# The last third of a gated MLP's down projection by seven block products, with the up tiles woven in another order

## The chip, the core and the metric

One core of a Trainium2 chip runs the whole kernel. The metric is device time in microseconds (us) of one execution. The median of three runs of the kernel before is 827.56 us (827.38 to 827.99). Engines go by their short names: PE is TensorE (matmul), DVE is VectorE, ACT is ScalarE, POOL is GpSimd, SP is SyncE, which issues most DMAs.

## The reference, cut to what matters

One inference step of a decoder layer: a mixer, cross-attention, then a gated MLP, and a final RMSNorm. The change lies in the MLP and the final norm. There are 512 prompt tokens and 8 sample tokens, 520 columns in all, held as two halves of 260.

```python
def conv_ffn(xn, prefix, w_up, conv_w, conv_b, w_down):
    up = xn @ w_up                      # 1024 -> 2 * 2816
    ext = jnp.concatenate([prefix, up], axis=1)
    c = conv_b
    for k in range(CONV_W): c = c + conv_w[k] * ext[:, k:k + T]     # causal, width 3
    gate, val = jnp.split(c, 2, axis=-1)
    return (jax.nn.silu(gate) * val) @ w_down, ext[:, -(CONV_W - 1):]   # 2816 -> 1024
```

## The kernel before, in words

Activations are held transposed, with 128 features on the partitions and 2 x 260 token columns. Every fp32 operand is split into two fp32r parts, hi (ACT, a copy that rounds) and lo (DVE, the difference: `split`, lines 117 and 120), and a product is three matmuls: hi.hi, hi.lo, lo.hi. Nearly every matmul is 128 x 128 weights against 260 columns.

The hidden layer has 22 tiles of 128 features (`FT`). An up tile j gives gate and value for both halves. Tiles 0 to 6 are **classic**: 8 blocks of the contraction, three matmuls each, two halves, two outputs, 96 matmuls. Tiles 7 to 21 go by **seven products** (`up_seven`, line 1870): gate and value, even and odd contraction blocks, and the two halves of the tokens form a 2 x 2 by 2 x 2 block product, done as seven block products instead of eight, 84 matmuls. The operands are sums of weight blocks and sums of activation blocks. The activation sums are made once (`mixes`, line 1738) and read through `xm`. Of the weight sums, two per tile are added by an accumulating DMA from POOL's queue (`both`, line 1877) and two by DVE (`sum2`, `sum4`, lines 1924 and 1929), each as the first thing of a later product's preparation. After the products, an up tile runs through `conv` (line 1674: two ACT and three DVE instructions) and `gate` (line 1689: Silu on ACT, gate times value on DVE, then the hi and lo split of the hidden tile).

The down projection reads the hidden tiles in three parts, `PARTS = ((0, 7), (7, 15), (15, FT))`, for each of 8 output blocks d (`down`, line 1859): classic, and added to the residual `hT` by DVE (line 1864). Parts 0 and 1 are placed between up tiles, one block d to an up tile, the rest behind the last one. Part 2 ends the stage: blocks d = 0 to 3 as `last_down` (line 1969), which also squares the finished block into an accumulator (`add_square`: ACT, then POOL, lines 274 and 276) and scales it (`final_block`); blocks 4 to 7 in the tail (lines 2055 to 2092), half by half, so that the first half's norm (`half_norm`) and stores (`half_store`) run beside the second half's matmuls.

The order is a list of `Step`s, written out by hand (lines 1941 to 1980). A step is a weight unit of up to 4 blocks (512 columns): loaded up to 13 steps ahead by SP into a ring of 13 raw units, split (`prep`) 3 steps ahead into a ring of 4 split units, and multiplied. In the seven-product stretch a step is 12 matmuls. After each step, two pieces of the deferred `conv` and `gate` work are issued (`POPS`, line 2007). Within each engine a list scheduler at build time orders ready instructions by priority, which is program order unless raised.

PSUM has three double banks `pp` and two single ones `t`. An up tile by seven products holds one `pp` and one `t`. The four outputs are read while products are still added: for instance product 6 adds onto the bank that products 1 and 5 left and that `keep` (line 1898) copies out first.

The `for m` loop from line 1991 drives it:

```python
    for m in range(-AHEAD, len(steps)):
        while loaded < min(m + EARLY, len(loads)) and loads[loaded].load():
            loaded += 1
        ...
        if m + AHEAD < len(steps):
            steps[m + AHEAD].prep()
        ...
        steps[m].mm()
        for _ in range(POPS):
            ...
```

Of the kernel before, what the change touches and what calls it, by code (L numbers as in the profile page):

```python
# [9 lines left out]
F32 = mybir.dt.float32  # L10
# [22 lines left out]
FT = DFF // P  # L33
MEM = 256
# [73 lines left out]
def decoder_step(ctx: ExitStack, tc: tile.TileContext, A, O):  # L108
# [1514 lines left out]
    w_up = A["w_up"][0]  # L1623
    w_down = A["w_down"][0]
    PARTS = ((0, 7), (7, 15), (15, FT))
    NA = PARTS[1][0]
    hid = {}
    hid_mid = []
    xs3 = blocks(x3_hi, x3_lo)
# [14 lines left out]
    def up_cols(v, j):  # L1644
        return slice(v * DFF + j * P, v * DFF + (j + 1) * P)

    def up_products(j):

        raws = [raw_w[j % 2][:, 2 * v:2 * v + 2].rearrange("p u (k c) -> p (u k) c", c=P) for v in range(2)]
        for v in range(2):  # L1650
            sp.dma_start(raws[v], w_up[:, up_cols(v, j)].rearrange("(k p) c -> p k c", p=P))
# [37 lines left out]
    def gate(j):  # L1689
# [6 lines left out]
        yield  # L1696
        tt(g, g, u, OP.mult)
        yield
        if NA <= j < PARTS[2][0]:
            if not hid_mid:  # L1700
                hid_mid.extend(ptile(ab3, [P, KT, 2, HT], t, F32R, name="h_mid") for t in ("x3_hi", "x3_lo"))
            hid[j] = tuple(t[:, j - NA] for t in hid_mid)
        else:
            hid[j] = tuple(ptile(ff, [P, 2, HT], t, F32R, bufs=7) for t in ("h_hi", "h_lo"))
# [25 lines left out]
    NI = KT // 2  # L1730
    xm4 = [ptile(actp, [P, 4, NI, HT], "act_a", F32R, bufs=2, name="xm4") for _ in range(2)]
    xm3 = ptile(ff, [P, 2, 3, NI, HT], "xm3", F32R)
    B11, B21, B22, T3_, N1, N2, T4_ = range(7)
# [25 lines left out]

    mix = mixes()  # L1760
# [28 lines left out]
    class Step:  # L1789

        def __init__(self, mm, load=None, prep=None, post=None, held=False):
            self.load_, self.prep_, self.mm_, self.post_, self.held = load, prep, mm, post, held
# [11 lines left out]
        def prep(self):  # L1804
            raw = self.prep_() if self.prep_ else self.raw
            if self.load_ and not self.held:
                self.free()
            n = raw.shape[1]
            self.w = tuple(t[:, :n] for t in ring_units(1))
            split(self.w[0], self.w[1], raw)  # L1810

        def mm(self):
            self.mm_(self.w)
            if self.post_:
                self.post_()

    def classic(ps_of, src, xs, kt, post):

        out = []
        for k0 in range(0, kt, 4):  # L1820
# [11 lines left out]
            out.append(Step(mm, load=lambda k0=k0, n=n: load_unit(rows(src, k0, n), n), post=post if k0 + n == kt else None))  # L1832
# [12 lines left out]
    def up_classic(j):  # L1845
        out = []
        for v in range(2):
# [8 lines left out]
            out.append(classic(ps, w_up[:, up_cols(v, j)], xs3, KT, post))  # L1856
        return out[0] + out[1]

    def down(pi, d, then=None):
# [8 lines left out]
        return classic(ps, w_down[j0 * P:j1 * P, d * P:(d + 1) * P], lambda k: hid[j0 + k], j1 - j0, post)  # L1868

    def up_seven(j):  # L1870

        ac, bb = held("pp"), held("t")

        def block(m, s):
            return w_up[:, up_cols(m, j)].rearrange("(i s p) c -> p s i c", s=2, p=P)[:, s]
# [38 lines left out]

        def out21():
            acopy(exts[j][:, 1, 0, 2:], a_of(False), scale=-1.0)
            behind.extend((conv(j, 1), gate(j)))

        s = {}
        s[1] = Step(product(a_of, B11, True), lambda: load_unit(block(0, 0)), held=True)  # L1920
        s[5] = Step(product(c_of, N1, True), both(block(1, 0), block(1, 1)), post=keep, held=True)
        s[2] = Step(product(b_of, B21, True), lambda: load_unit(block(0, 1)), post=out11, held=True)

        def sum2():
            tt(s[1].raw, s[1].raw, s[5].raw, OP.add)
            s[5].free()
            return s[1].raw

        def sum4():
# [244 lines left out]
```

## Time and profile before

| | |
|---|---|
| median of three runs | 827.56 us (827.38 to 827.99) |
| the profiled execution's own time | 827.17 us |
| its span, first to last instruction | 825.5 us |
| granted clock of PE, mean | 0.996 |
| PE / DVE / ACT busy, share of the span | 98% / 73% / 54% |
| matmuls | 6891 |

The busy share says how long an engine had something in it. Whether an engine sets the end is read from the chain of waits and from how fast its instructions follow one another. "L1890" is line 1890 of the kernel; a line of a helper (117, 120) stands for many uses, which the tile names tell apart.

### The profile page before, as it was taken

To read this page: it belongs to the slowest core of one execution; us is meant where nothing else is said; L and a number is where in the kernel's file an instruction comes from. 1 tells how busy PE (TensorE), PEld (TensorE's weight loads), DVE (VectorE), ACT (ScalarE), POOL (GpSimd) and SP (SyncE) were. 2 spreads that over 40 slices of the span, in tenths; PEclk is the share of its full clock that TensorE was granted. 3 is DMA by queue.
4 is the path that set the end of the run, shared out by engine and by line. 5 is a ranking of instruction groups with operands and counts; after the bars stand their busy time and mean duration, and the time that the engine had idled before them with its cause. 6 is when DMAs were issued, how large, how long until landed. Compare 5 with 4: busy or idle time off the path is not lost.

```text
span 825.5 us, 17791 instructions
## 1 busy us (share of the span) xinstructions
PE 808.3 (98%) x6891; PEld 753.7 (91%) x6891; DVE 605.2 (73%) x1460; ACT 447.9 (54%) x940; POOL 95.3 (12%) x100
## 2 busy tenths in 40 slices
PE   9999999899999999999999999999999999999996
PEld 8998878877778899999799999999999999999995
DVE  6644686887657776888673799997888887887714
ACT  6741347667665553444343465666666656665541
POOL 2300111000000031000032000111111111100021
PEclk9999999999999999999999999999999999999998
DMA  9988975833222283677443224756866866754422
GB/s 327 304 257 289 411 285 182 270 115 116 77 77 53 64 254 106 202 251 254 137 115 103 77 78 126 154 134 152 165 143 147 168 145 142 160 135 121 171 110 104
DMA packets 146366, 137.87 MB, mean 167 GB/s; under 512 B 6417, under 2 KB 133265, under 8 KB 144089
## 3 DMA queue, kind: packets, MB, share of 16 engines
q1 hardware_dynamic: 127224, 114.63, 44.5%
q0 software_dynamic: 18624, 21.26, 12.0%
q8 instruction: 54, 0.88, 0.4%
q10 hardware_dynamic: 432, 0.84, 0.3%
q14 instruction: 32, 0.25, 0.1%
HBM read 129.56 MB, written 10.69 MB: 170 GB/s over the span
## 4 chain that ended last, share of the span: by engine, by line
PE 90%; DVE 3%; ACT 3%; DMA 2%; issue 1%; SPq 0%; DVEq 0%; ACTq 0%
PE ps_pp L205 29%; PE ps_pp L1890 16%; PE ps_pp L1829 16%; PE ps_t L1890 3%; PE ps_tb L1266 3%; PE ps_o L1155 2%; PE ps_pp L2070 2%; PE ps_tb L1072 2%; PE ps_sc L1108 2%; PE ps_tf L1140 2%; PE ps_x L1467 1%; PE ps_tb L1234 1%; PE ps_x L1488 1%; ACT prob L1118 1%; PE ps_s L1528 1%
## 5 line engine op out<-in xcount | busy, mean ns | idle before, releaser
L1890 PE MATMUL ps_pp<-xm,w_hi 128*128 128x260 f32 x720 | 133.3, 285 | 0.0
L1890 PEld LDWEIGHTS ps_pp<-xm,w_hi 128*128 128x128 f32 x720 | 110.9, 188 | 2.3 <-ACT ext L117 0.2
L117 ACT ACTIVATE w_hi<-w_u 128x512 fp32r<-128x512 f32 (+2 forms) x110 | 72.7, 661 | 66.4 <-PE ps_pp L1890 22.7
L1890 PE MATMUL ps_pp<-xm,w_lo 128*128 128x260 f32 x360 | 101.5, 282 | 0.0
L120 DVE TENSOR_TENSOR w_lo<-w_u,w_hi 128x512 fp32r<-128x512 f32 (+2 forms) x110 | 80.1, 729 | 16.6 <-ACT w_hi L117 15.3
L1890 PEld LDWEIGHTS ps_pp<-xm,w_lo 128*128 128x128 f32 x360 | 67.7, 188 | 0.0
L120 DVE TENSOR_TENSOR hT<-hT,ps_pp 128x520 f32<-128x520 f32 (+1 forms) x44 | 28.4, 645 | 45.0 <-PE ps_pp L205 17.9
L205 PE MATMUL ps_pp<-x_hi,w_hi 128*128 128x260 f32 x288 | 59.9, 286 | 0.0
L205 PE MATMUL ps_pp<-x_hi,w_lo 128*128 128x260 f32 x288 | 59.6, 285 | 0.0
L205 PE MATMUL ps_pp<-x_lo,w_hi 128*128 128x260 f32 x288 | 58.5, 284 | 0.0
L117 ACT ACTIVATE w_hi<-w_raw 128x1024 fp32r<-128x1024 f32 (+1 forms) x38 | 35.1, 922 | 41.3 <-PE ps_pp L205 30.0
L1118 ACT ACTIVATE prob<-prob,mx 128x384 f32<-128x384 f32 (+3 forms) x64 | 35.4, 555 | 19.3 <-DVE mx L1116 19.1
L120 DVE TENSOR_TENSOR w_lo<-w_raw,w_hi 128x1024 fp32r<-128x1024 f32 (+1 forms) x38 | 41.4, 1089 | 6.1 <-ACT w_hi L117 5.8
L205 PEld LDWEIGHTS ps_pp<-x_hi,w_lo 128*128 128x128 f32 x288 | 44.9, 188 | 0.6 <-issue 0.4
L205 PE MATMUL ps_pp<-xn_hi,w_hi 128*128 128x260 f32 x208 | 45.1, 291 | 0.2 <-issue 0.2
L205 PEld LDWEIGHTS ps_pp<-x_hi,w_hi 128*128 128x128 f32 x288 | 44.9, 188 | 0.3
L1880 POOL DMA_DIRECT2D w_u<-in_w_up_dram x19 | 24.4, 1286 | 178.9 <-DMA w_u<-in_w_up_dram 106.8
L205 PEld LDWEIGHTS ps_pp<-x_lo,w_hi 128*128 128x128 f32 x288 | 44.4, 188 | 0.4 <-issue 0.4
L120 DVE TENSOR_TENSOR w_lo<-raw_x,w_hi 128x512 fp32r<-128x512 f32 (+1 forms) x53 | 35.7, 674 | 10.3 <-ACT w_hi L117 9.6
L205 PE MATMUL ps_pp<-xn_lo,w_hi 128*128 128x260 f32 x208 | 42.9, 285 | 0.3 <-DVE xn_lo L129 0.3
L205 PE MATMUL ps_pp<-xn_hi,w_lo 128*128 128x260 f32 x208 | 43.0, 286 | 0.0
L117 ACT ACTIVATE w_hi<-raw_x 128x512 fp32r<-128x512 f32 (+1 forms) x53 | 32.8, 618 | 18.1 <-PE ps_pp L1890 13.1
(495 smaller groups left out, 2309.8 us busy)
## 6 DMA issues: line engine op xcount, KB each, us to landing
w_u<-in_w_up_dram SPq DMA_DIRECT2D x57, 256.0 KB, 3.2
xkr<-in_cache_mem_dram SPq DMA_DIRECT2D x16, 512.0 KB, 4.7
xvr<-in_cache_mem_dram SPq DMA_DIRECT2D x16, 512.0 KB, 7.1
raw_x<-in_w_up_dram SPq DMA_DIRECT2D x26, 256.0 KB, 3.4
Kt<-in_k_t_dram SPq DMA_DIRECT2D x48, 128.0 KB, 3.2
w_u<-in_w_up_dram SPq DMA_DIRECT2D x10, 512.0 KB, 4.3
w_u<-in_w_down_dram SPq DMA_DIRECT2D x20, 256.0 KB, 4.4
w_u<-in_w_up_dram POOLq DMA_DIRECT2D x19, 256.0 KB, 5.8
```

The source lines that it names most:

```text
L117: act.activation(o, i, AF.Copy, scale=scale)
L120: (eng or dve).tensor_tensor(o, a, b, op=op)
L205: pe.matmul(o, a[:, k, :], x[:, hf, :], start=(k == 0 and j == 0), stop=(k == kt - 1 and j == 2))
L1072: pe.matmul(ps[:, :HT], a[:, k, :], y[x][:, k, hf, :], start=(k + j == 0), stop=(k == 3 and j == 2))
L1108: pe.matmul(ss_[hl][:, 0:n], Qst[:, h, qc], k[:, g, u, 0:n], start=(u == 0), stop=(u == 1), skip_group_check=True)
L1118: act.activation(p[:, 0:nk], p[:, 0:nk], AF.Exp, bias=mx[:, hh:hh + 1], scale=-1.0, accum_out=sm[:, hh:hh + 1])
L1140: pe.transpose(pt[:, hh * P:(hh + 1) * P], pr[hh][:, kb * P:(kb + 1) * P], ident)
L1155: pe.matmul(po[hp * 64:(hp + 1) * 64, g * 256:(g + 1) * 256], Vtok[:, br, kb, g * 64:(g + 1) * 64], pTs[kb][:, hp * 256:(hp + 1) * 256], s ...
L1266: pe.matmul(ps[i], x[:, k, ts_], w[:, kl, :], start=(k == 0 and j == 0), stop=(k == KT - 1 and j == 2))
L1829: pe.matmul(ps[:, hf, :HT], a[:, k, :], x[:, hf, :], start=(k0 + k + j == 0), stop=(k0 + k == kt - 1 and j == 2))
L1880: pool.dma_start(u[1], b, accum_op=OP.add)
L1890: pe.matmul(ps, a[:, i, :], b, start=(first and i + q == 0), stop=(i == NI - 1 and q == 2), skip_group_check=True)
```

## The change

- The down projection's parts become (0, 7), (7, 14), (14, 22). Its last part, eight hidden tiles, goes by seven products for output blocks 0 to 5, in three pairs (`down_seven`); blocks 6 and 7 stay classic, in the tail.
- Hidden tiles 14 to 21 are kept unsplit (`raw_hid`); `hidden_mixes` makes their block sums and the hi and lo parts, in pieces of four per step behind the up tiles.
- The steps of the up tiles are woven so that products of three tiles alternate (`weave`); `keep` joins `out11`; results are read out under high priority; the down blocks of part 0 stand with the first eight tiles, three of part 1 within the last tile, five behind it.
- The weight sums by DVE (`add`) follow the split of their own unit (`after`) instead of opening a later preparation. The accumulating DMAs are issued up to five steps after the load (`LATER`). The flag `dma`, which would give the other sums to POOL's queue as well, is False in both uses.
- The weights of up and down are laid out on the host so that a unit is one contiguous run per partition.
- The tail has two blocks instead of four; its weights are split in the last four steps; the first half's norm comes after the fourth contraction block of d = 6, its stores within d = 7. Three copies of cache and state from DRAM to DRAM (lines 1996 to 1999) wait until no accumulating DMA is left. Three pieces of deferred work follow a step instead of two.

The diff, cut to its core:

```diff
+PARTS = ((0, 7), (7, 14), (14, FT))
+DOWN_ORDER = list(range(14)) + list(range(14, FT, 2)) + list(range(15, FT, 2))
...
-    PARTS = ((0, 7), (7, 15), (15, FT))
-    xs3 = blocks(x3_hi, x3_lo)
+    def xs3(k):
+        kk = 2 * (k % NI) + k // NI
+        return x3_hi[:, kk], x3_lo[:, kk]
...
+        if j >= NB2:
+            if not raw_hid:
+                raw_hid.append(ptile(ff, [P, KT, 2, HT], "hA", name="raw_hid"))
+            tt(raw_hid[0][:, j - NB2], g, u, OP.mult)
+            yield
+            return
...
+        for i in range(NI):
+            e, o = raw_hid[0][:, 2 * i], raw_hid[0][:, 2 * i + 1]
+            both = raw_hid[0][:, 2 * i:2 * i + 2].rearrange("p s r t -> p r s t")
+            at_ = [t[:, :, i].rearrange("p (r s) t -> p r s t", r=2) for t in blk]
+            acopy(at_[0], both)
+            yield
+            n, t = (ptile(ff, [P, 2, HT], "cv", bufs=3, name="hz") for _ in range(2))
+            tt(n[:, 0], e[:, 0], e[:, 1], OP.subtract)
+            yield
+            tt(t[:, 0], o[:, 1], e[:, 1], OP.subtract)
+            yield
+            dve.scalar_tensor_tensor(n[:, 1], n[:, 0], -1.0, o[:, 1], op0=OP.mult, op1=OP.subtract)
+            acopy(mid[:, 0, 2, i], t[:, 0])
+            yield
+            dve.scalar_tensor_tensor(t[:, 1], n[:, 1], -1.0, o[:, 0], op0=OP.mult, op1=OP.subtract)
+            acopy(mid[:, 0, 0:2, i], n)
+            yield
+            tt(at_[1], both, at_[0].bitcast(F32), OP.subtract)
+            acopy(end[:, 0, i], t[:, 1])
+            yield
+            tt(mid[:, 1, 0:2, i], n, mid[:, 0, 0:2, i].bitcast(F32), OP.subtract)
+            yield
+            tt(mid[:, 1, 2, i], t[:, 0], mid[:, 0, 2, i].bitcast(F32), OP.subtract)
+            yield
+            tt(end[:, 1, i], t[:, 1], end[:, 0, i].bitcast(F32), OP.subtract)
...
             split(self.w[0], self.w[1], raw)
+            if self.after:
+                self.after()
 
         def mm(self):
             self.mm_(self.w)
             if self.post_:
-                self.post_()
+                with tc.high_priority():
+                    self.post_()
...
-                pool.dma_start(u[1], b, accum_op=OP.add)
+                adds.append([LATER, u[1], b])
...
         def sum2():
-            tt(s[1].raw, s[1].raw, s[5].raw, OP.add)
             s[5].free()
             return s[1].raw
 
         def sum4():
-            tt(s[2].raw, s[2].raw, s[1].raw, OP.add)
             s[1].free()
             s[2].free()
             return s[2].raw
 
-        s[6] = Step(product(a_of, N2, False), prep=sum2, post=lambda: acopy(exts[j][:, 0, 1, 2:], a_of(False)))
-        s[3] = Step(product(c_of, B22, False), prep=sum4, post=out12)
-        s[7] = Step(product(a_of, T3_, False), both(block(0, 0), block(1, 0)), post=out22)
-        s[4] = Step(product(a_of, T4_, False), lambda: load_unit(block(1, 1)), post=out21)
+        s[1] = Step(product(a_of, B11, True), lambda: load_unit(block(0, 0)), held=True)
+        s[5] = Step(product(c_of, N1, True), both(block(1, 0), block(1, 1)), held=True, after=lambda: add(1, 5))
+        s[2] = Step(product(b_of, B21, True), lambda: load_unit(block(0, 1)), post=posts[2], held=True, after=lambda: add(2, 1))
+        s[6] = Step(product(a_of, N2, False), prep=sum2, post=posts[6])
+        s[3] = Step(product(c_of, B22, False), prep=sum4, post=posts[3])
+        s[7] = Step(product(a_of, T3_, False), both(block(0, 0), block(1, 0)), post=posts[7])
+        s[4] = Step(product(a_of, T4_, False), lambda: load_unit(block(1, 1)), post=posts[4])
...
+        def add(m, r, x, op=OP.add):
+            tt(hT[:, d + m, r], hT[:, d + m, r], x(), op)
+
+        def first():
+            add(0, 0, a)
+            add(1, 1, c, OP.subtract)
+            add(0, 0, b)
+
+        def done():
+            add(1, 0, a, OP.subtract)
+            then(d)
+            then(d + 1)
+
+        posts = {2: first, 6: lambda: add(0, 1, a), 3: lambda: add(0, 1, c), 7: lambda: add(1, 1, a, OP.subtract), 4: done}
+        return seven(lambda m, s: w_down[d + m, :, NB2 + NI * s:NB2 + NI * s + NI], hm, ac, bb, posts, False)
...
-    steps += [sevens[0][i] for i in (1, 5, 2, 6, 3)]
-    for n, s in enumerate(sevens):
-        t = sevens[n + 1] if n + 1 < len(sevens) else None
-        if n:
-            steps += downs.pop(0)
-        if not t:
-            steps += [s[7]] + downs.pop(0) + [s[4]]
-        elif n:
-            steps += [s[7], t[1], t[5], s[4], t[2], t[6], t[3]]
-        else:
-            steps += [t[1], t[5], s[7], t[2], s[4], t[6], t[3]]
+    steps += [sevens[0][i] for i in (1, 5, 2)]
+    def weave(rows, places, last):
+
+        prev = None
+        for n, s in enumerate(rows):
+            t = rows[n + 1] if n + 1 < len(rows) else None
+            seq = ([s[6], t[1]] if prev and t else [t[1], s[6]] if t else [s[6]]) + ([prev[4]] if prev else [])
+            if t:
+                seq += [s[3]] + (downs.pop(0) if n in places else []) + [t[5], t[2], s[7]]
+            else:
+                seq += last() + [s[3]] + last() + [s[7]] + last() + [s[4]]
+            steps.extend(seq)
+            prev = s
+
+    weave(sevens, (0, 1, 2, 3, 4, 5, 6, 7), lambda: downs.pop(0))
+    ups_end = len(steps)
...
-    D0 = 4
-        steps += last_down(d)
+    D0 = 6
+    groups = [down_seven(q, down_done) for q in range(D0 // 2)]
+    steps += [groups[0][i] for i in (1, 5, 2)]
+    weave(groups, (), lambda: [])
...
-    AHEAD, EARLY, POPS = 3, 13, 2
+    AHEAD, EARLY, POPS = 3, 13, 3
...
+        soon = [s.raw for s in steps[max(m + AHEAD, 0):m + AHEAD + 4] if hasattr(s, "raw")]
+        for e in list(adds):
+            e[0] -= 1
+            if e[0] <= 0 or any(e[1] is r for r in soon):
+                adds.remove(e)
+                pool.dma_start(e[1], e[2], accum_op=OP.add)
         if m + AHEAD < len(steps):
             steps[m + AHEAD].prep()
         if m < 0:
             continue
+        if loaded == len(loads) and not adds and kept:
+            for o, i in kept:
+                with last_on(EN.SP):
+                    sp.dma_start(o, i)
+            kept = ()
...
+        if m >= ups_end:
+            for _ in range(4):
+                next(hidden, None)
+        if m >= len(steps) - 4 and hasattr(tail_raw[-1], "raw"):
+            tail_split(m - len(steps) + 4)
...
+                if hf == 1 and (d, k) == (D0, 4):
+                    stores = half_store(0, half_norm(0, sq0))
+                    lead = last_pe()
+                if hf == 1 and d == D0 + 1 and k in (1, 3, 5):
                     next(stores)
-                xhi, xlo = hid[j0 + k]
...
-            if hf == 1:
-                if d == D0:
-                    stores = half_store(0, half_norm(0, sq0))
...
+    given["w_up_t"] = x["w_up"][0].reshape(4, 2, P, 2, FT, P).transpose(3, 4, 2, 1, 0, 5)
+    given["w_down_t"] = x["w_down"][0].reshape(FT, P, KT, P).transpose(2, 1, 0, 3)[:, :, DOWN_ORDER]
```

## Rows read from the trace of the kernel before

**Rows 1.** The page, part 1: busy time of an engine, its share of the span, and its instructions.

```profile
PE 808.3 (98%) x6891; PEld 753.7 (91%) x6891; DVE 605.2 (73%) x1460; ACT 447.9 (54%) x940; POOL 95.3 (12%) x100
```

**Rows 2.** The chain that ended last, in order of time, in the MLP: start us, length us, what, and how many matmuls. Of the pieces like the one at 564.95 there are thirteen, one to an up tile, the last at 752.24. The last row is the end of the matmuls of the tail, but for the norm's.

```profile
536.60 7.37 PE ps_pp L1890 x60
...
545.41 3.14 PE ps_pp L1890 x24
...
549.54 1.71 PE ps_pp L1890 x12
...
562.55 1.45 PE ps_pp L1890 x12
...
564.95 1.63 PE ps_pp L1890 x12
...
752.24 1.64 PE ps_pp L1890 x12
...
767.29 25.89 PE ps_pp L1829 x216
...
809.38 5.76 PE ps_pp L2070 x48
```

**Rows 3.** Busy time of each engine in three stretches: three up tiles, each with a down block of 48 matmuls; the end of the up tiles with two more; and the classic last part before the tail. Columns: stretch, its length, then PE, PEld, DVE, ACT, POOL busy us (instructions), granted clock, DMA share, GB/s.

```profile
690.57:738.60 48.03, 48.03 (x398) 47.61 (x397) 39.55 (x70) 29.31 (x61) 6.44 (x5) 1.00 0.67 147
738.60:767.30 28.70, 28.70 (x240) 28.56 (x239) 20.68 (x36) 15.01 (x30) 0.00 (x0) 1.00 0.38 110
767.30:793.20 25.90, 25.90 (x218) 25.90 (x218) 13.79 (x24) 13.14 (x28) 4.43 (x4) 1.00 0.50 197
```

**Rows 4.** All groups of DVE instructions in the first of these stretches (690.57 to 738.60, three up tiles), by shape: count, busy us, mean ns of one, and the idle time before them with what ended it.

```profile
L120 DVE TENSOR_TENSOR w_lo<-w_u,w_hi 128x512 fp32r<-128x512 f32 x15 | 10.3, 690 | 4.1 <-ACT w_hi L117 3.8
L120 DVE TENSOR_TENSOR w_lo<-raw_x,w_hi 128x512 fp32r<-128x512 f32 x12 | 8.3, 688 | 0.9 <-ACT w_hi L117 0.8
L1682 DVE SCALAR_TENSOR_TENSOR cv<-ext,taps,cv 128x512 f32<-128x512 f32 x6 | 4.5, 749 | 0.0
L1684 DVE SCALAR_TENSOR_TENSOR cv<-ext,taps,cv 128x512 f32<-128x512 f32 x6 | 4.5, 745 | 0.0
L120 DVE TENSOR_TENSOR h_lo<-cv,h_hi 128x520 fp32r<-128x520 f32 x4 | 2.8, 694 | 0.0
L120 DVE TENSOR_TENSOR hT<-hT,ps_pp 128x520 f32<-128x520 f32 x3 | 2.1, 697 | 1.2 <-PE ps_pp L1829 1.2
L120 DVE TENSOR_TENSOR cv<-cv 128x520 f32<-128x520 f32 x3 | 2.1, 692 | 0.0
L120 DVE TENSOR_TENSOR raw_x<-raw_x 128x512 f32<-128x512 f32 x3 | 2.1, 688 | 0.0
L120 DVE TENSOR_TENSOR w_u<-w_u 128x512 f32<-128x512 f32 x2 | 1.4, 688 | 0.0
L1913 DVE SCALAR_TENSOR_TENSOR ext<-ps_pp,ext 128x260 f32<-128x260 f32 x3 | 1.3, 429 | 0.4
L120 DVE TENSOR_TENSOR ext<-ext,ps_pp 128x260 f32<-128x260 f32 x3 | 1.3, 426 | 1.2 <-PE ps_pp L1890 1.2
L120 DVE TENSOR_TENSOR ext<-ext,ps_t 128x260 f32<-128x260 f32 x3 | 1.3, 426 | 0.5 <-PE ps_t L1890 0.5
L120 DVE TENSOR_TENSOR cv<-cv,base 128x8 f32<-128x8 f32 x6 | 1.0, 166 | 0.0
L120 DVE TENSOR_TENSOR w_u<-w_u,raw_x 128x512 f32<-128x512 f32 x1 | 0.7, 693 | 0.0
```

**Rows 5.** From the same view of 486 to 556 us: the shapes that `mixes` uses, and a split of three blocks.

```profile
L120 DVE TENSOR_TENSOR xm<-raw_x,xm 128x1040 fp32r<-128x1040 f32 x3 | 3.7, 1234 | 0.0
...
L120 DVE TENSOR_TENSOR raw_x<-raw_x 128x260 f32<-128x260 f32 x6 | 2.5, 424 | 0.0
...
L120 DVE TENSOR_TENSOR w_lo<-raw_x,w_hi 128x384 fp32r<-128x384 f32 x1 | 0.6, 560 | 0.2 <-ACT w_hi L117 0.2
```

**Rows 6.** Instructions in order of time, POOL's and DVE's, in an earlier stage that also squares finished blocks: start us, length us, engine, instruction. The second line's split runs beside the first line's POOL addition, the fifth's beside the fourth's.

```profile
418.29 1.39 POOL L276 TENSOR_TENSOR acc<-acc,sq 128x520 f32<-128x520 f32 x1 [2.42 <-ACT sq L274]
418.69 1.54 DVE L120 TENSOR_TENSOR w_lo<-w_raw,w_hi 128x512 fp32r<-128x512 f32 x1 [0.18 <-ACT w_hi L117]
...
420.75 0.68 DVE L120 TENSOR_TENSOR w_lo<-w_raw,w_hi 128x512 fp32r<-128x512 f32 x1
...
422.20 1.36 POOL L276 TENSOR_TENSOR acc<-acc,sq 128x520 f32<-128x520 f32 x1 [2.53 <-ACT sq L274]
...
422.90 1.21 DVE L120 TENSOR_TENSOR w_lo<-w_raw,w_hi 128x512 fp32r<-128x512 f32 x1 [0.51 <-ACT w_hi L117]
```

**Rows 7.** Two DVE groups of the tail (793.2 to the end) by shape, as in rows 4.

```profile
L120 DVE TENSOR_TENSOR hg<-hg,ps_t 128x780 f32<-128x780 f32 x4 | 3.8, 964 | 1.7 <-PE ps_t L2048 1.7
...
L120 DVE TENSOR_TENSOR hg<-hg,ps_t 128x520 f32<-128x520 f32 x2 | 1.4, 690 | 0.0
```

**Rows 8.** The copy of 4 MB from DRAM to DRAM: its issue by SP, from the instructions in order of time.

```profile
772.03 0.84 SPq L1996 DMA_DIRECT2D out_win_keep_dram<-in_cache_win_dram  x1
```

**Rows 9.** Busy time of each engine in two stretches after that issue (columns as in rows 3).

```profile
784.00:796.00 12.00, 12.00 (x102) 12.00 (x101) 1.95 (x4) 4.22 (x9) 3.88 (x3) 1.00 0.47 200
796.00:808.00 12.00, 12.00 (x102) 12.00 (x101) 2.29 (x8) 5.62 (x13) 2.45 (x5) 1.00 0.01 2
```

**Rows 10.** The page, part 6: issues of an accumulating DMA from POOL's queue, KB each, median us from issue to landing.

```profile
w_u<-in_w_up_dram POOLq DMA_DIRECT2D x19, 256.0 KB, 5.8
```

More of the change, by code (lines that the diff above doesn't have):

```diff
@@ L1703, in gate @@
         else:
-            hid[j] = tuple(ptile(ff, [P, 2, HT], t, F32R, bufs=7) for t in ("h_hi", "h_lo"))
+            if not hid_ends:
+                end_tiles()
+            hid[j] = tuple(t[:, j] for t in hid_ends)
         acopy(hid[j][0], g)
@@ L1805, in prep @@
             raw = self.prep_() if self.prep_ else self.raw
+            assert all(o is not raw for _, o, _ in adds)
             if self.load_ and not self.held:
@@ L1830, in mm @@
                                       stop=(k0 + k == kt - 1 and j == 2))
-            out.append(Step(mm, load=lambda k0=k0, n=n: load_unit(rows(src, k0, n), n), post=post if k0 + n == kt else None))
+            out.append(Step(mm, load=lambda k0=k0, n=n: load_unit(src[:, k0:k0 + n], n), post=post if k0 + n == kt else None))
         return out
@@ L1866, in post, with seven @@
                 then()
[L1868 to L1875, printed above, removed]
+        return classic(ps, w_down[d, :, j0:j1], lambda k: hid[j0 + k], j1 - j0, post)
+    LATER = 5
+    adds = []
+    def seven(block, mixed, ac, bb, posts, dma):
         def both(a, b):
@@ L1990, in decoder_step, with tail_split @@
     loaded = 0
+    wl = []
+    def tail_split(u):
+        if u in tail_done:
+            return
+        tail_done.add(u)
+        if not wl:
+            wl.extend(ptile(ab3, [P, KT, 2, HT], t, F32R, name="wl").rearrange("p a r t -> p (a r t)")
+                      [:, 0:(KT - D0) * kt * P].rearrange("p (d k c) -> p d k c", k=kt, c=P) for t in ("x3_hi", "x3_lo"))
+        dl, k0 = u // 2, u % 2 * 4
+        split(*(t[:, dl, k0:k0 + 4] for t in wl), tail_raw[u].raw)
+    tail_done = set()
+    hidden = hidden_mixes()
+    kept = [(O["win_keep"].rearrange("b t c g d -> b t (c g d)"), A["cache_win"][0, :, 1:WIN].rearrange("b t c g d -> b t (c g d)")),
+            (O["pool_keep"], A["state_pool"][0, :, 1:15, :]), (O["ffn_keep"], A["state_ffn"][0, :, 1, :])]
     for m in range(-AHEAD, len(steps)):
@@ L2015, in decoder_step @@
         run(g)
-    assert loaded == len(loads)
-    wl_hi, wl_lo = (ptile(ab3, [P, KT, 2, HT], t, F32R, name="wl").rearrange("p a r t -> p (a r t)")
-                    [:, 0:(KT - D0) * kt * P].rearrange("p (d k c) -> p d k c", k=kt, c=P) for t in ("x3_hi", "x3_lo"))
+    assert loaded == len(loads) and not adds
+    for u in range(2 * (KT - D0)):
+        tail_split(u)
+    wl_hi, wl_lo = wl
     eps_d = ptile(ff, [P, 1], "eps_d")
@@ L2056, in decoder_step @@
     stores = iter(())
+    lead = None
     for hf in range(2):
@@ L2080, in decoder_step @@
             todo.append(lambda d=d, hf=hf: final_block(d, (hf,)))
-            if hf == 1:
-                if d == D0:
-                    stores = half_store(0, half_norm(0, sq0))
-                elif d > D0 + 1:
-                    next(stores, None)
         sq0 = sq
```

133 lines of the change are left out of this document (76 added, 57 removed).

## The prediction

> **What bounds the kernel now.** I read the page's busy shares first, then the chain of waits in order of time, then the busy time by stretch, then DVE's instructions in one stretch. The shares: PE 98%, DVE 73%, ACT 54% [rows 1]. [...]
>
> What PE loses is small and regular. In each later up tile one product takes 1.63 us where its neighbour takes 1.45 (twelve matmuls by 0.1199 are 1.44): 13 pieces by 0.19, 2.5 us [rows 2]. The entry into the weave loses 7.37 - 60 x 0.1199 = 0.18, 3.14 - 24 x 0.1199 = 0.26 and 1.71 - 1.44 = 0.27, together 0.7 us [rows 2]. That is all: 3.2 us.
>
> The second engine is DVE. In three up tiles with their down blocks it is busy 39.55 of 48.03 us [rows 3], while the durations of its 70 instructions add to 43.7 us [rows 4]: neighbours overlap, and one costs its duration less (43.7 - 39.55) / 70 = 0.06 us when they follow closely. I call that its pitch: 0.63 for a split or a sum of 512 columns, 0.37 for a 260-column read from PSUM, 0.69 and 0.69 for the two long steps of `conv`, 0.11 for its short one, 0.63 for the gate's product [rows 4]. ACT is busy 29.31 us there [rows 3], 9.8 a tile; without a down block's two splits and the hidden tile's hi copy, some 0.6 each, that is 8.0. I cost ACT's edits at nothing; their cover is the fifth of the time that this leaves it even in a tile of 10.1 us, and without it each of its copies would delay the DVE half of a split.
>
> **Matmuls removed.** Three pairs of blocks at 84 instead of 96 matmuls: 36 by 0.1199 are **-4.3 us**. The other parts only move a tile from part 1 to part 2; the count of the rest is the same.
>
> **Stalls of the old weave.** The late product is the one that adds onto a bank which the read-out of the product just before it still holds: in the old order 2, 6, 3 of a tile follow one another. The new order puts another tile's product or a down block between each read-out and the next product on that bank, and raises the read-outs' priority. I take the 13 pieces as gone, **-2.5 us**, and leave the 0.7 of the entry; bounds: nothing gained, or 3.2.
>
> **Up tiles without a down block.** Six tiles (the ninth to the fourteenth of fifteen) now have no down block. There PE needs 84 x 0.1199 = 10.1 us a tile. DVE needs seven splits (4.4), two sums (1.3), two `conv` (2 x 1.49 = 3.0), the gate's product (0.6; these tiles are kept unsplit) and three read-outs (1.1): 10.4 us. DVE is 0.3 us a tile behind, 1.8 us over six. It begins with three steps split ahead, 3 x 1.44 = 4.3 us, so most of this is swallowed. I take **+1.0 us**; bounds 0 (the lead swallows all) and, with every instruction at full duration, 11.5 us a tile: 6 x 1.4 - 4.3 = 4.1.
>
> **Five down blocks with the hidden mixes.** PE: 210 matmuls, 25.2 us. DVE: the last tile's second `conv` and its gate 2.1; seven of ten splits 3.9 (0.63, or 0.50 for three blocks [rows 5]); five adds to hT 3.2; three preparations and two sums for the first pair 3.2; and the mixes, per pair of tiles four differences of 260 (1.5), one lo part of 1040 (1.17), one of 520 (0.63) and two of 260 (0.73) [rows 4, 5], 4.0, four times 16.0. Sum 28.3, so 3.1 behind. The mixes also start late: their scratch shares three buffers with `conv`, and the last tile must be through it.
>
> **The three pairs.** PE: 252 matmuls, 30.2 us. DVE: 21 splits and 6 sums at 0.63 and 21 adds to hT at 0.37 are 24.8, less the 3.2 already done, plus four tail splits 2.5: 24.1. On top come POOL's additions. Four of them now fall where DVE is busy, and the trace shows what that does: beside a POOL addition a split took 1.54 or 1.21 us instead of 0.68 [rows 6], on average 0.7 more; 2.8 us for four. With the 3.1 left over, DVE has 30.0 to do in 30.2. I take **+2.0 us** for both stretches, because work that only just fits arrives late somewhere; bounds 0 and 6. [...]
>
> **Edits that I cost at nothing.** *The sums behind their own split*: same count and kind, only earlier. The first of them waits for the accumulated unit, and queued behind it on DVE is the next split; but the split just before it reads the same unit, so the wait is not new. *Accumulating DMAs later*: they still lie five steps (7.2 us at 1.44) or, rarely, three before the preparation, and three further steps before PE; a landing takes 5.8 us [rows 10]. POOL's queue carries additions and the store of `last` as well, but the accumulates are issued ahead of those. With that cover gone each late one would stall PE by its lateness. *Contiguous weights*: loads were never in the chain of this stage; nothing or a little gain. *DRAM to DRAM copies*: issued by SP at 772 before [rows 8], with the DMA share down from 0.47 to 0.01 by 796 to 808 [rows 9], so at most some 24 us long. Now, counted through the loop, nine steps before the pairs end: 9 x 1.44 + 96 tail matmuls x 0.12 + the 10.4 us behind the last large matmul (809.38 + 5.76 against a span of 825.5 [rows 2]) are 35 us before the end. They still fit, ahead of the stores on SP's queue. *Three pieces of deferred work a step*: order only.
>
> **Tail.** Removed matmuls are counted above. The first half's norm now comes 36 matmuls (4.3 us) before the last one, its three scalings (2 x 0.96 + 0.69 = 2.6 us [rows 7]) within the last 2.5 us; the last block's add to hT then waits behind one of them: **+0.4 us**, bounds 0 and 1.
>
> **Sum.** -4.3 - 2.5 + 1.0 + 2.0 + 0.4 = -3.4. Against the profiled execution's 827.17 (span 825.5, 1.7 around it, unchanged) that is 823.8; the median of the runs stands 0.4 higher, so **824.1 us**. A measurement of this kernel tells about 0.2% from no change, 1.7 us: the limits are 825.9 and 829.2.
>
> **Rivals.**
> *A, PE stays the only bound.* DVE's lead swallows all. For it: deficits of 1.8 and 3.1 us against leads of 4.3. Against: no stretch of rows 3 has DVE above 82%, so nothing shows it at 100 [rows 3]. -4.3 - 3.2 + 0 to 0.4: 820 to 820.5.
>
> *B, the stalls only change their place.* The 1.63 us pieces come back under another step, since banks and read-outs are as many; DVE's lateness comes as forecast. -4.3 + 3.0 + 0.4 = -0.9, 826.7: no change. For it: three tiles now share three `pp` banks, and each down block needs one of the three.
>
> *C, DVE becomes the bound: slower.* If a full queue gives no overlap, each instruction costs its whole duration. Six tiles then lose 4.1 beyond the lead; the same sums as above at whole durations give 31.5 for 25.2 in the next stretch and 29.7 for 30.2 in the pairs, 5.8 more. +4.1 + 5.8 + 0.4 - 4.3 - 2.5 = +3.5: 831.1. Between my 3.0 of new stalls at a pitch of 0.63 and these 9.9 at 0.69, the gain is gone at some 0.66. Against it: 39.55 busy for 43.7 [rows 3, 4]. [...]
>
> *D, an edit that isn't there*: no sum of weights changes its engine, since `dma` is False and the accumulating DMAs stay; I count nothing for that, so it changes no number.
>
> **Chances.** Forecast 0.50 (822 to 825.9), A 0.25, B 0.14, C 0.11. Faster 0.75, within 0.2% 0.14, slower 0.11. The range leaves out C and little else: 820.0 to 827.3.
>
> **What the profile will show.** 6855 matmuls. If right: no piece of 1.63 us at a fixed place in the up tiles; DVE above 95% in the six tiles without down blocks, with short PE waits for `w_lo`; PE gaps of 1 to 3 us between the last up tile and the second pair. If PE has no gap there, A. If PE waits for `w_lo` for over 1 us in each of the six tiles, C. What would make it all wrong is a wait that I have not priced: a bank or an accumulate that is late in every tile.

## The result and the profile after

The kernel after takes **820.28 us** (median of 6 runs, 819.76 to 822.66) against 827.77 in runs of the kernel before beside it: ratio 0.991, 95% interval [0.9896, 0.9924], 7.5 us less. A repeat gave 819.94 against 826.81, ratio 0.9913 [0.9892, 0.9934], 6.9 us less. The forecast was 3.4 us less, so the sign and the range held, and the size was less than half of what came.

The profiled execution of after took 822.66 us, span 821.0. It stands above its median because of time lost before 165 us, in a stage that the change doesn't touch: its list of steps starts 2.3 us later than before's, while in the profile of the repeat (819.11 us) it starts 0.9 us earlier. So I measure the **MLP stretch**, from the first matmul of the list of steps (up tile 5; the up tiles before it run ahead of the list, with equal matmuls in both kernels) to the last 260-column matmul of the tail, both by their starts: 305.78 us before, 299.20 after, 299.18 in the repeat. That is 6.58 less; what follows the stretch went from 10.68 to 10.43. Together 6.8 us, close to the 6.9 and 7.5 of the medians; the small rest lies ahead of the stretch and in the scatter of the runs.

The page, part 1, of after [rows 1]:

```profile
PE 801.4 (98%) x6855; PEld 747.7 (91%) x6855; DVE 623.3 (76%) x1512; ACT 457.7 (56%) x955; POOL 87.5 (11%) x104
```

The chain of waits of after, columns as in [rows 2]:

```profile
542.57 1.62 PE ps_pp L1955 x12
...
558.35 5.04 PE ps_pp L1896 x42
563.39 1.44 PE ps_pp L1955 x12
564.83 1.45 PE ps_t L1955 x12
566.27 7.19 PE ps_pp L1955 x60
...
656.96 8.62 PE ps_pp L1955 x72
665.58 1.45 PE ps_t L1955 x12
667.03 8.62 PE ps_pp L1955 x72
...
741.14 25.13 PE ps_pp L1896 x210
...
771.97 0.64 ACT w_hi L119
...
772.63 0.70 DVE w_lo L122
...
785.61 1.53 POOL acc L278
...
790.52 0.62 ACT w_hi L119
...
791.15 3.14 PE ps_pp L1955 x24
794.29 0.60 PE ps_pp L2199 x5
...
794.90 1.69 PE ps_pp L1955 x12
...
808.34 2.53 PE ps_pp L2199 x21
...
810.89 0.43 DVE hT L122
```

Sixty matmuls in a row take 7.19 us, 0.1198 each: the old pieces of 1.63 are gone, and of the entry's loss one piece is left (1.62, 0.18 over). The six tiles without a down block run at 8.62 + 1.45 = 10.07 us with no other engine in the chain, and so do the five down blocks. Between the entry and the tail only the pairs have ACT, DVE and POOL in the chain. PE's gaps there, beyond the usual pitch of its matmuls, are 0.32 us at 774.1, 0.38 at 790.7, and 0.26 each at 794.6 and 796.9: 1.2 us.

Busy time by stretch, columns as in [rows 3]: one and six tiles without a down block, the end of the up tiles, the five down blocks, the pairs.

```profile
667.03:677.10 10.07, 10.07 (x86) 10.07 (x86) 10.04 (x20) 7.87 (x18) 1.72 (x2) 1.00 0.67 165
656.96:717.39 60.43, 60.43 (x506) 60.43 (x506) 58.52 (x111) 46.48 (x102) 7.75 (x9) 1.00 0.68 166
717.39:741.14 23.75, 23.75 (x201) 23.75 (x200) 19.65 (x34) 14.48 (x28) 0.86 (x1) 1.00 0.53 146
741.14:766.26 25.12, 25.12 (x212) 25.12 (x212) 23.61 (x50) 13.03 (x28) 3.98 (x5) 1.00 0.65 147
766.26:798.90 32.64, 32.40 (x265) 31.66 (x264) 25.77 (x47) 20.04 (x37) 7.33 (x6) 1.00 0.44 146
```

DVE is busy 97% of six tiles, as forecast, and yet PE has no gap there. The granted clock is 1.00 in all of them, so none of the difference is clock.

### The profile page after: what moved, and what is told of

The parts are those of the page before. It is cut to its first block, busy times and chain, and to the rows that moved or that the text cites. A ratio compares the mean times of both kernels' runs of the same rounds, so it can differ in the third digit from the quotient of the medians.

```text
span 821.0 us, 17806 instructions
## 1 busy us (share of the span) xinstructions
PE 801.4 (98%) x6855; PEld 747.7 (91%) x6855; DVE 623.3 (76%) x1512; ACT 457.7 (56%) x955; POOL 87.5 (11%) x104
## 4 chain that ended last, share of the span: by engine, by line
PE 84%; DVE 5%; DMA 4%; ACT 4%; issue 2%; POOL 0%; SPq 0%; DVEq 0%; ACTq 0%; POOLq 0%
PE ps_pp L207 25%; PE ps_pp L1955 18%; PE ps_pp L1896 13%; PE ps_t L1955 3%; PE ps_tb L1268 3%; PE ps_o L1157 2%; PE ps_tb L1074 2%; PE ps_sc L1110 2%; PE ps_tf L1142 2%; DMA out_kv_t_dram<-ztile 1%; PE ps_x L1469 1%; PE ps_pp L2199 1%; PE ps_tb L1236 1%; PE ps_x L1490 1%; ACT prob L1120 1%
## 5 line engine op out<-in xcount | busy, mean ns | idle before, releaser
L1955 PE MATMUL ps_pp<-xm,w_hi 128*128 128x260 f32 x720 | 130.7, 282 | 0.0
L119 ACT ACTIVATE w_hi<-w_u 128x512 fp32r<-128x512 f32 (+2 forms) x117 | 76.5, 655 | 73.8 <-PE ps_pp L1955 25.9
L122 DVE TENSOR_TENSOR w_lo<-w_u,w_hi 128x512 fp32r<-128x512 f32 (+2 forms) x117 | 84.5, 726 | 15.5 <-ACT w_hi L119 15.1
L122 DVE TENSOR_TENSOR hT<-hT,ps_pp 128x520 f32<-128x520 f32 (+1 forms) x54 | 31.2, 582 | 30.1 <-PE ps_pp L207 17.9
L119 ACT ACTIVATE w_hi<-raw_x 128x512 fp32r<-128x512 f32 (+1 forms) x59 | 36.7, 622 | 21.9 <-PE ps_pp L1955 14.2
L122 DVE TENSOR_TENSOR w_lo<-raw_x,w_hi 128x512 fp32r<-128x512 f32 (+1 forms) x59 | 40.1, 685 | 7.9 <-ACT w_hi L119 7.7
L1896 PE MATMUL ps_pp<-h_mid,w_hi 128*128 128x260 f32 x224 | 36.0, 282 | 0.0
```

What stands on the lines that cost most here:

```text
L119: act.activation(o, i, AF.Copy, scale=scale)
L122: (eng or dve).tensor_tensor(o, a, b, op=op)
L1896: pe.matmul(ps[:, hf, :HT], a[:, k, :], x[:, hf, :], start=(k0 + k + j == 0), stop=(k0 + k == kt - 1 and j == 2))
L1955: pe.matmul(ps, a[:, i, :], b, start=(first and i + q == 0), stop=(i == NI - 1 and q == 2), skip_group_check=True)
```

## Experiments

**One part alone.** *Order only*: before with the new weave, read-outs at high priority, sums behind their split and accumulates issued later; classic last part and old layout. *Layout only*: before with the new weights' layout. *Old order*: after, with the old sequence of products of the up tiles and `keep` behind product 5 again; high priority, sums and accumulates stay as in after. The lines that decide:

```diff
 order only (against before)
-    steps += [sevens[0][i] for i in (1, 5, 2, 6, 3)]
+    steps += [sevens[0][i] for i in (1, 5, 2)]
+    weave(sevens, (0, 1, 2, 3, 4, 5, 6, 7), lambda: downs.pop(0))
...
 layout only (against before)
-    w_up = A["w_up"][0]
...
+    w_up = A["w_up_t"]
...
 old order (against after)
-    weave(sevens, (0, 1, 2, 3, 4, 5, 6, 7), lambda: downs.pop(0))
...
+        if t:
+            steps += [s[7], t[1], t[5], s[4], t[2], t[6], t[3]]
```

> The kernel before with the new order of steps alone (weave, read-outs under high priority, sums behind their own split, accumulating DMAs later, three deferred pieces a step); parts (0,7), (7,15), (15,22), all classic, old weight layout, old tail. Theory 1 (PE stays the only bound; a matmul removed is worth 0.12 us and the order takes away the regular 0.19 us stalls): 6891 matmuls stay, the 13 late products and most of the entry's loss go, about -3.0 us, so 824.7, and no 1.63 us piece in the chain. Theory 2 (DVE full in the six tiles without a down block at 10.4 us a tile, as the prediction priced it): -2.0, some 825.8, with waits for w_lo in those tiles. If the order is worth nothing: 827.7, the stalls somewhere else.

> The kernel before with nothing but the weights of up and down laid out as one contiguous run per partition. Theory 1: loads are not in the chain of this stage, so 827.7, within 0.5 us of before, with fewer DMA packets (about 79,000 in place of 146,000). Theory 3 (a part of the 7.5 us comes from faster loads): 0.5 to 1.5 us faster, with the chain before the MLP shorter by that.

> The changed kernel with the old order of the products of the up tiles (7, 1, 5, 4, 2, 6, 3 of two neighbours, keep behind product 5), down blocks at the same tiles as in the changed kernel, all else as changed. Theory 1 (the late product waits for the bank that the read-out before it still holds): a piece of about 1.63 us in place of 1.44 once a tile, 14 tiles, +2.6 us against the changed kernel, about 822.9; where no down block follows the scheduler has less to fill the gap with, so up to 0.5 a tile there, +4.5. Rival (the stalls went away by high priority alone): 820.3 as the changed kernel.

| against 827.01 | median us | ratio to before | MLP stretch us |
|---|---|---|---|
| order only | 826.10 | 0.9987 [0.9974, 0.9999] | 304.30 |
| layout only | 826.72 | 0.9998 [0.9982, 1.0014] | 305.62 |
| old order | 826.94 | 0.9996 [0.9980, 1.0012] | 306.44 |

The layout is worth nothing that the whole time can show, though the kernel's 137.87 MB then move in 77,629 DMA packets instead of 146,366; in the stretch it is 0.16 us, all of it in the first 192 matmuls, which start 0.1193 us apart instead of 0.1201. The order alone gives 1.5 us of the stretch; all of after with the old sequence loses 0.7, and after as it is gains 6.6: the parts are not additive. Old order also lets the rival fall that high priority alone removes the stalls, and costs more than both figures expected, 7.2 us: five of the six tiles without a down block lose 0.9 us each and the first 0.5, where a tile with one loses 0.19 as before, and the pairs lose 0.75 more. In the six tiles PE and its weight loads wait for ACT's copies of a bank; the view of waits of that kernel from 655 to 720 us (engine, line, released by, us in total, times, longest) says so:

```profile
PEld ps_pp L1955 <- ACT ext L119: 3.2, 5, 0.6
PE ps_pp L1955 <- ACT ext L119: 2.1, 5, 0.4
```

With the order only, the thirteen pieces are gone and the entry keeps 0.18 us, as in after. But those six tiles still split their hidden tile, one instruction more each for DVE (and one for ACT), and lose 1.0 us in all, and the last up tile 0.5: so 1.5 is left of 3.0, and 826.10 is above both figures expected (824.7 and 825.8).

**How late may DVE be?** Three kernels, after with n of the seven lo parts computed a second time in each of the six tiles without a down block (n = 1, 2, 4): more work for DVE and nothing else. The comment in the diff below is not in the kernels.

```diff
             split(self.w[0], self.w[1], raw)
+            if getattr(self, "twice", False):
+                tt(self.w[1], raw, self.w[0].bitcast(F32), OP.subtract)
...
+    for j in range(15, 21):
+        for k in (1, 7):        # n = 2; (5,) for n = 1, (1, 5, 2, 7) for n = 4
+            sevens[j - NA][k].twice = True
```

> The changed kernel with one lo part per tile computed twice in the six up tiles without a down block (0.60 us more of DVE a tile, same output). From four doubled parts DVE's need is 9.85 + 0.603 us per doubled part and PE's is 10.08. One part: 10.45, so 0.37 us a tile behind, 2.2 over six. If the lead of the split steps is worth 2 to 3 us, as the pattern of gaps with two and four parts says, it swallows nearly all of it: MLP stretch 299.2 to 299.6 us. If there is no lead: 301.4 us. This is also the tile that the prediction forecast (10.4 us of DVE), so it says whether the forecast of +1.0 us followed from that size.

> The changed kernel with two of the seven splits of six up tiles (the ninth to the fourteenth by seven products) doing their lo part twice, the same values again: 1.2 us more of DVE a tile. Theory 1 with the pitch that the full queue showed (duration less 0.08, 9.75 to 10.0 us a tile of 10.08, lead 4.3 us): DVE wants 11.0 to 11.2, is 0.9 to 1.1 behind a tile, 5.5 to 6.6 over six, less the lead: +1.2 to +2.3, so 821.5 to 822.6. Theory 2 (pitch 0.63, 10.4 a tile): 1.5 behind a tile, 9.3, less 4.3: +5, 825.3. No lead at all: +5.5 to 6.6.

> The changed kernel with four lo parts per tile computed twice in the six up tiles without a down block (2.4 us more of DVE a tile, the output is the same). If DVE needs 9.75 us a tile in the changed kernel (the run with two doubled parts fits that) and PE 10.08, and the lead of three split steps swallows nothing, each tile loses 9.75 + 2.4 - 10.08 = 2.1 us, six tiles 12.4: MLP stretch 299.2 + 12.4 = 311.6 us. If the prediction's lead of 4.3 us is real: 12.4 - 4.3 = 8.1, 307.3. If the prediction's 10.4 us a tile were right as well as its lead: 6 x 2.7 - 4.3 = 12.0, 311.2, but then the run with two doubled parts would have lost 5.0 with its largest gaps in the last tiles alone, not in each.

| n | MLP stretch us | more than after | time, one run (n = 2: median of 10) |
|---|---|---|---|
| 0 | 299.20 | | |
| 1 | 300.28 | 1.1 | 821.47 |
| 2 | 304.26 | 5.1 | 826.27, ratio to before 0.9989 [0.9973, 1.0004] |
| 4 | 308.95 | 9.8 | 831.22 |

Busy time by stretch (columns as in [rows 3]), of n = 4, n = 2 and n = 1 in this order, one tile each:

```profile
683.28:695.54 12.26, 10.90 (x85) 10.30 (x85) 12.26 (x25) 8.05 (x17) 1.72 (x2) 1.00 0.58 147
```

```profile
683.70:695.10 11.40, 10.61 (x85) 10.20 (x85) 11.20 (x23) 7.91 (x17) 0.90 (x2) 1.00 0.71 163
```

```profile
677.10:687.20 10.10, 10.10 (x87) 10.10 (x86) 10.10 (x20) 7.79 (x18) 2.14 (x3) 1.00 0.69 160
```

With n = 4 DVE never idles and a tile takes 12.26 us for 23 instructions: its true need. The pitch follows from DVE's instructions of after in order of time (start us, length us, what):

```profile
671.07 0.69 DVE L122 TENSOR_TENSOR w_lo<-w_u,w_hi 128x512 fp32r<-128x512 f32 x1
671.67 0.69 DVE L122 TENSOR_TENSOR raw_x<-raw_x,w_u 128x512 f32<-128x512 f32 x1
672.27 0.69 DVE L122 TENSOR_TENSOR w_lo<-w_u,w_hi 128x512 fp32r<-128x512 f32 x1
673.00 0.69 DVE L122 TENSOR_TENSOR w_u<-w_u,raw_x 128x512 f32<-128x512 f32 x1
...
674.25 0.42 DVE L122 TENSOR_TENSOR ext<-ext,ps_pp 128x260 f32<-128x260 f32 x1
674.60 0.75 DVE L1692 SCALAR_TENSOR_TENSOR cv<-ext,taps,cv 128x512 f32<-128x512 f32 x1
675.26 0.17 DVE L122 TENSOR_TENSOR cv<-cv,base 128x8 f32<-128x8 f32 x1
675.35 0.68 DVE L122 TENSOR_TENSOR w_lo<-raw_x,w_hi 128x512 fp32r<-128x512 f32 x1
```

From start to start, 0.60 us for 512 columns (671.07, 671.67, 672.27), 0.34 to 0.35 for a read-out, 0.66 for a long step of conv, 0.09 for the short one. The nineteen instructions of a tile are 10 x 0.60 + 3 x 0.34 + 4 x 0.66 + 2 x 0.09 = 9.84 us; with n more, 10.44, 11.04 and 12.24, which n = 4 confirms at 12.26. PE's 10.07 lies above 9.84: **DVE was never behind** in after. Where it is behind (n = 1: 0.37 a tile, 2.2 over six), the loss is 1.1. With n = 2 the lateness is 0.97 a tile, 5.8 over six, and the loss 5.1; with n = 4 it is 2.17 a tile, 13.0, and 9.8 are lost.

How much of it the lead of the split steps swallows is read from PE's gaps, tile by tile. With n = 4 they are 0.2, 1.7, three times 2.2, and 1.0 us, with 0.4 more in the last up tile: 2.4 us of lateness are swallowed in the first two tiles. With n = 2 they are 0, 0.7, 1.2, 1.3, 1.3 and 0.3, again with 0.4 in the last: 1.3 us are swallowed at first, and after that a tile loses more than its 0.97. In three of its tiles one split of DVE starts 0.28 us later than DVE's queue alone would let it, since it waits for a hi part of ACT that comes late behind PE; the chain of n = 2 shows the first of them:

```profile
683.75 2.55 PE ps_pp L1957 x19
...
686.32 0.65 ACT w_hi L119
...
686.99 0.69 DVE w_lo L122
```

With n = 1, 1.1 us are swallowed. So the lead is worth 1 to 2.4 us here; neither "no lead" nor a lead of 4.3 fits. The +5 of theory 2 for n = 2 is met in number alone: a tile of its 10.4 us with four more parts would take 12.8 us or more, not 12.26.

**The sums of the hidden tiles in program order.** After, with DVE and ACT held to program order for them.

```diff
-                next(hidden, None)
+                with last_on(EN.DVE, EN.Activation):
+                    next(hidden, None)
```

> The changed kernel with DVE and ACT held to program order for the sums of the hidden tiles, so that they can't be drawn ahead of the work around them. The prediction's reason (sums start late and leave DVE 2 to 3 us behind in the stretch of five down blocks): then 2 to 3 us of PE gaps appear in that stretch or before the first pair, MLP stretch 301.2 to 302.2 us. Rival (DVE has room there anyway, 23.6 of 25.1 us busy): the sums end later but PE loses less than 0.5 us, MLP stretch 299.2 to 299.7 us.

One run 819.97 us, MLP stretch 299.94, 0.74 more than after. By stretch, the five down blocks and then the pairs up to the third:

```profile
737.80:762.93 25.13, 25.13 (x212) 25.13 (x212) 23.65 (x47) 15.77 (x31) 4.00 (x5) 1.00 0.62 135
762.93:788.57 25.64, 25.15 (x204) 24.46 (x204) 25.53 (x48) 16.44 (x31) 5.11 (x4) 1.00 0.48 152
```

PE has no gap in the five down blocks; the work left over is done in the pairs, DVE fills 25.53 of 25.64 us there, and PE's gaps in the pairs add to 1.9 us instead of 1.2, the largest 0.73 at 787.8, where after has 0.38. In after, by contrast, three of the four wide lo parts (1040 columns, 1.24 us each) are done before the five blocks begin, as DVE's groups of 717.39 to 741.14 by shape show:

```profile
L122 DVE TENSOR_TENSOR hx_b<-raw_hid,hx_b 128x1040 fp32r<-128x1040 f32 x3 | 3.6, 1238 | 0.3 <-ACT hx_b L119 0.3
```

So the scheduler's early start is worth 0.7 us of the stretch, in one run of it. Both expectations missed: no loss of 2 to 3, and yet more than 0.5, in another place.

**The squares of finished blocks.** The square of block 0 is POOL's own; those of blocks 1 to 5 are ACT's, and POOL adds them to the accumulator. *Three buffers*: after, with a ring of three scratch buffers instead of one. *No squares*: after, without the squares of blocks 1 to 5, so that its output leaves these blocks out. The comment in the diff below is not in the kernel.

```diff
-        add_square(acc4, hT[:, d], d)
+        if d == 0:
+            add_square(acc4, hT[:, d], d)
+        else:                               # no squares: this branch is left out
+            sq = ptile(ff, [P, 2, HT], "cv", bufs=3, name="sqd")
+            act.activation(sq, hT[:, d], AF.Square)
+            pool.tensor_tensor(acc4, acc4, sq, op=OP.add)
```

> The changed kernel with the squares of the finished blocks in a ring of three scratch buffers instead of one, so that ACT need not wait for POOL's addition. Theory (POOL's additions delay ACT through the single buffer): the wait of 0.76 us of ACT at 787 and PE's gap of 0.38 us at 790.7 go, about 0.3 to 0.4 us off the three pairs, ratio to the changed kernel 0.9996, to the kernel before 0.990 to 0.991. Rival (the gap is DVE's, slowed by the addition itself): DVE's lo parts still take 1.0 to 1.3 us beside the additions and PE's gaps stay within 0.1 us.

> The changed kernel without the squares of output blocks 1 to 5, thus without five ACT squares and five POOL additions (the final norm then leaves these blocks out). Theory: the 1.2 us of PE gaps that remain in the three pairs come from POOL's additions; without them they fall below 0.3 us, the pairs take 32.64 - 1.0 = 31.6 us, and no DVE instruction of 512 columns in the pairs lasts over 0.8 us. Rival: they come from DVE's or the units' own order; then at least 0.8 us of gaps stay.

POOL, DVE and ACT of after in order of time:

```profile
785.61 1.52 POOL L278 TENSOR_TENSOR acc<-acc,sq 128x520 f32<-128x520 f32 x1 [7.80 <-ACT sq L276]
787.87 1.31 POOL L278 TENSOR_TENSOR acc<-acc,sq 128x520 f32<-128x520 f32 x1 [0.75 <-ACT sq L276]
```

```profile
786.43 1.25 DVE L122 TENSOR_TENSOR w_lo<-raw_x,w_hi 128x512 fp32r<-128x512 f32 x1
...
788.76 0.98 DVE L122 TENSOR_TENSOR w_lo<-w_u,w_hi 128x512 fp32r<-128x512 f32 x1 [0.41 <-ACT w_hi L119]
```

```profile
787.16 0.64 ACT L276 ACTIVATE sq<-hT 128x520 f32<-128x520 f32 x1 [0.76 <-POOL acc L278]
```

The same two splits without the squares:

```profile
783.19 0.69 DVE L122 TENSOR_TENSOR w_lo<-raw_x,w_hi 128x512 fp32r<-128x512 f32 x1
...
784.46 0.68 DVE L122 TENSOR_TENSOR w_lo<-w_u,w_hi 128x512 fp32r<-128x512 f32 x1
```

An addition by POOL lengthens a split by 0.56 and 0.30 us here, and both go when the additions go: this is shown. (A third split, at 777.34, takes 1.02 us beside POOL's own square of block 0; without the other squares that one stays, and so does its length, 1.01.) Without the squares the MLP stretch is 298.78 (one run, 819.30 us), 0.4 less: the gap at 790.7 is gone, those at 774, 794 and 797 stay. So they are not the additions', and the theory that all 1.2 us come from them fell. With three buffers the same gap shrinks to 0.08 us though the splits are still long:

```profile
783.30 1.27 DVE L122 TENSOR_TENSOR w_lo<-raw_x,w_hi 128x512 fp32r<-128x512 f32 x1
...
785.16 1.13 DVE L122 TENSOR_TENSOR w_lo<-w_u,w_hi 128x512 fp32r<-128x512 f32 x1
```

So ACT's wait for the one buffer (0.76 us before 787.16, with the next split's hi part queued behind it) made the gap, not DVE's length. The stretch is 298.88, and 298.80 in a repeat beside the kernel after:

> The changed kernel once more, unchanged, beside the one with three scratch buffers for the squares: MLP stretch within 0.2 us of 299.2, ratio to the kernel before 0.990 to 0.993.

> The changed kernel with three scratch buffers for the squares, on the same chip as the changed kernel. If the 0.3 us that its MLP stretch was shorter count in the whole, its median is 0.2 to 0.5 us below that of the changed kernel; the runs scatter by more than that, so the whole time may show nothing and the MLP stretch (298.9 against 299.2 us) decides.

| | median us | ratio to before | MLP stretch us |
|---|---|---|---|
| after, repeat | 819.94 | 0.9913 [0.9892, 0.9934] | 299.18 |
| three buffers, first | 819.15 | 0.9924 [0.9910, 0.9937] | 298.88 |
| three buffers, repeat | 819.09 | 0.9897 [0.9876, 0.9919] | 298.80 |

In the stretch it is 0.3 to 0.4 us better both times. In the whole time the intervals overlap, so that three buffers beat the kernel after is likely and not shown.

## Why the prediction was right and wrong

| term | forecast | measured |
|---|---|---|
| 36 matmuls | -4.3 | -4.3 (36 x 0.1198) |
| stalls of the old weave and the entry | -2.5 | -3.0 |
| six tiles without a down block | +1.0 | 0.0 |
| five down blocks and three pairs | +2.0 | +1.2, all in the pairs |
| tail | +0.4 | -0.25 |
| matmuls' own spacing | 0 | -0.4 (gaps over 0.02 us left out: 0.1199 us before, 0.1197 after, 2486 times) |
| sum | -3.4 | -6.8 |

**What held.** The matmuls are priced as one can read them: before, 216 one after another took 0.1199 us each (767.29 in [rows 2]) and PE was busy from end to end in the stretches of [rows 3]; after, sixty took 0.1198 each. The stalls of 0.19 left with the order, and even the entry kept only 0.18 of its 0.7. None of the edits costed at nothing shows a cost, the layout (tried alone) among them. The forecast that DVE would stand above 95% in the six tiles came true, but without the limit that it was a sign of; the two signs beside it failed: PE has no wait for `w_lo` in these tiles, and 0.32 us of gaps up to the second pair instead of 1 to 3.

**The step that failed** is the price of a DVE instruction, my pitch of duration minus 0.06. I took it as an average over a stretch where DVE idled 18% of the time [rows 3, 4]: a neighbour that comes late doesn't overlap (in after the instruction at 672.27 lasts 0.69 us and the next starts 0.73 us after it), so the average overlap is too small and the price too high. It had to be read from two starts that follow one another. The trace of before had them, in DVE's instructions in order of time:

```profile
690.84 0.69 DVE L120 TENSOR_TENSOR w_lo<-raw_x,w_hi 128x512 fp32r<-128x512 f32 x1
691.44 0.74 DVE L1682 SCALAR_TENSOR_TENSOR cv<-ext,taps,cv 128x512 f32<-128x512 f32 x1
...
704.20 0.68 DVE L120 TENSOR_TENSOR w_lo<-w_u,w_hi 128x512 fp32r<-128x512 f32 x1
704.80 0.69 DVE L120 TENSOR_TENSOR cv<-cv 128x520 f32<-128x520 f32 x1
```

They give 0.60, and 9.84 us a tile instead of 10.4: below PE's 10.07 instead of above it. That one sign makes the term +1.0 into 0. The rest of the step was sound: a tile that does need 10.44 us (n = 1) loses 1.1 us over six, where I had forecast 1.0. That agreement is partly luck: I had 1.8 us of lateness and a lead of 4.3, by which all of it would have been swallowed, and took +1.0 by judgement; measured are 2.2 us of lateness, of which 1.1 are swallowed. The pitch is the largest single miss, not the whole of the 3.4 us between forecast and measurement: the six tiles are 1.0 of it, the blocks and pairs 0.8 (the pitch in part), the entry, which I left at nothing gained, 0.5, the tail 0.65 (no gain, as below, but no loss either), and the spacing of the matmuls 0.4, whose cause is open but for the 0.16 that come with the layout.

**Five down blocks and pairs.** The pitch takes 50 x 0.025 = 1.3 us off the 28.3. My reason that the sums start late was wrong: three wide lo parts, 3.6 us, are done before the five blocks begin, and the early start is worth 0.7. The additions by POOL were priced at 2.8 us of DVE time; POOL's square of block 0 and two additions that met a long DVE instruction (777.34, 786.43 and 788.76) cost it 0.34 + 0.56 + 0.30 = 1.2 us, and the others met none. Where a split met one of them, the added time is what is left of POOL's instruction when DVE's begins, less some 0.13 us: at 777.34 0.47 us are left of the square that began at 776.76 and lasts 1.05, and the split is 0.34 longer; at 786.43 0.70 us are left of the addition that began at 785.61 and lasts 1.52, and it is 0.56 longer; at 788.76 0.42 are left, and it is 0.30. The two rows of [rows 6] follow it too (0.99 left and 0.85 longer, 0.66 and 0.52). The runs show this price and that, for the two additions, it goes with them; by what means POOL's instruction holds DVE's up is not shown. Of the 1.2 us of gaps, 0.4 belong to the single buffer of the squares. What makes the gap at 774.1 was not tried (the chain names ACT's hi part behind PE, then DVE's lo part, a sum and a read-out), nor were the two of 0.26 in the last pair, each of which ends some 0.15 us after a read-out by DVE: that is open.

**Tail.** In the chain the last add to hT follows PE at once (810.89, 0.02 us after PE's last piece): the three scalings that it was to wait behind do stand ahead of it, but start at 808.38 and are done at 810.82, 2.44 us where I had 2.6 from whole durations. Runs with after's tail give 10.15 to 10.52 us for the end, and the two with the old tail, order only and layout only, 10.31 and 10.32, so the 0.25 is not a gain either.

**The rivals.** A (820 to 820.5) is what came, though not by its reason: there was no lateness for a lead to swallow in the six tiles, and it has no place for the 1.2 us of gaps in the pairs. That 820.28 lies in its range is in part luck: the spacing and the scatter of the whole time make up for them. B fell, no piece of 1.6 us stands in the up tiles. C fell with the pitch: at 12.26 us for 23 instructions DVE does overlap under a full queue, more than I assumed. One of 512 columns lasts 0.69 us, and the next starts 0.60 us after it.

## What to carry to other kernels

Price an engine that comes close to its limit by start-to-start times of instructions that really follow one another, never by busy time over a stretch in which it idles: here that price decided the sign, DVE's 9.84 us a tile (priced at 10.4) against PE's 10.07. DVE's busy share of 97% in the six tiles did not show a bound: double one instruction and see whether the next engine moves. Test the parts of a change in both directions, alone and left out, since an order and the work that it arranges may be worth little apart (1.5 us of the stretch by the order alone, 0.7 lost without it, 6.6 gained together).

## What the runs showed that I had not expected

- DVE's busy time overstates its need. In the tile of 667.03 it is busy 10.04 of 10.07 us while its need is 9.84: each instruction lasts 0.69 us even when the next starts 0.73 us later (672.27, 673.00), so up to 0.09 us of slack an instruction counts as busy.
- The six tiles run with 0.23 us a tile to spare. One more DVE instruction of 0.60 us in each costs 1.1 us in all, two cost 5.1, most of the gain. That the hidden tiles are kept unsplit, one DVE instruction less, is thus likely part of why the change pays: with the order only, where they are split, the six tiles lose 1.0 us. No run splits them in after itself.
- Nearly halving the number of DMA packets changed the whole time by nothing that these runs can show (ratio 0.9998 [0.9982, 1.0014]).
